# The last layer's final normalization, moved beside the last two experts of a mixture-of-experts encoder

## The chip, the core and the metric

The kernel runs on one core of a Trainium2 chip. A core has a matrix engine (PE, with its weight loads PEld), a vector engine (DVE), a scalar engine (ACT), a general engine (POOL) and a queue for transfers (SP), each with an instruction queue of its own that runs in order; sixteen DMA engines move data between memory and the core. Times are microseconds (us). The metric is the device time of one execution. Of the profile, the span reaches from the first to the last instruction.

## What is computed

Two layers of an encoder over 1024 tokens of 1024 features. Each layer is a mixer, a layer norm, a mixture of experts with 16 experts of which every token takes two, and another layer norm. What matters here is the end of the second layer:

```python
x = layer_norm(ALPHA * x + mixed @ w_out[i], ln_g[i, 0], ln_b[i, 0])
x = layer_norm(ALPHA * x + moe(x, ...), ln_g[i, 1], ln_b[i, 1])
# moe, per expert e and its tokens: (silu(xb @ w_gate[e]) * (xb @ w_up[e])) @ w_down[e], times the token's weight, summed per token
```

## The kernel before

`tail(layer, ...)` is the end of a layer: the output projection, the experts (`moe`), a loop for experts with more tokens than their places (`moe_rest`, none in this run's trace), and in the last layer `last_norm`, the final layer norm.

`moe` runs over the experts in the order 0, 8, 1, 9, ... 7, 15 (`SEQ`). Experts 0 to 7 have places for 192 tokens, a main part of 128 (`la`, `xa`, `ya`) and an extra part of 64 (`lb`, `xb`, `yb`); experts 8 to 15 have 128. For an expert its tokens' rows are gathered from memory (`gather`), transposed on PE and split into a high and a low part (`xah`, `xal`, and `xbc` for the extra part), multiplied with the gate and up weights (`gate_up`, PSUM tiles `dense`), passed through silu and the product on ACT and DVE (`ha`, `hb`), transposed again (`hposes`, tile `rtr`, then `hah`, `hal`, `hbc`), and multiplied with the down weights (`down`, PSUM tiles `rlg`, two buffers). ACT scales the result by the tokens' weights (`ya`, L2249; DVE for `yb`), and POOL issues an accumulating scatter of these rows into `accd` in memory (L2251, L2270), which already holds ALPHA * x. Each scatter waits for the one before it. `expert_weights` streams 1 MB weight tiles through SP into four raw buffers (`w_raw`); ACT and DVE split each (L77, L78) into one of five pairs `w_hi`, `w_lo`. PE works on expert n's gate and up weights and then on expert n-1's down weights; so the end of the program's work on PE is gate and up of expert 15, down of expert 7 (main, then extra part), down of expert 15. `late` holds the evacuations that `flush()` issues after the next matmuls; `rest` holds a generator of which each `flush()` runs one step (before: only the sorting of the routes).

`last_norm` runs `moe_norm`, which plans eight tiles of 128 tokens on the engines by estimated costs. All eight tiles are loaded from `accd` (L2370). Tiles 0 and 2: statistics on DVE (L2402 to L2406), reciprocal deviation on POOL (L2430), mean and deviation applied on ACT (L2441), times ln_g and plus ln_b on POOL (L2444, L2447). The other six: sums on ACT (L2410 to L2421), variance and reciprocal deviation on POOL (L2425, L2430), and two fused passes on DVE (L2435, L2438). SP stores each tile (L2467).

## Time and profile before

| | us |
|---|---|
| median of three runs | 2092.78 (2091.72 to 2098.09) |
| the profiled execution: its time | 2094.94 |
| the profiled execution: its span | 2093.2 |
| last matmul of the last expert begins | 2041.52 |
| last accumulating scatter has landed | 2053.6 (2047.12 + 6.49) |
| last fused pass of the final norm ends | 2089.4 |

Over the whole span PE is busy 90%, DVE 69%, ACT 53%, POOL 30%. A number of a row is the start on the chip's clock from the beginning of the span, then a duration. A row's idle time is that of the row's engine just before it.

### The profile page before, as it was taken

What the parts mean: (1) busy time and instruction counts of PE and PEld (TensorE: products, weight loads), DVE (VectorE), ACT (ScalarE), POOL (GpSimd) and SP (SyncE); (2) the same over time, 40 slices, a digit from 0 to 9 for tenths busy, and PEclk for the clock granted to TensorE, in tenths of its full rate; (3) what the DMA queues carried; (4) which work ended last, traced back from release to release, by engine and by line L of the source; (5) the groups of instructions that cost most, each with busy time, mean ns of one, the idle gap of its engine ahead of it and who ended that gap; (6) DMA issues with size and microseconds to landing.
All of it is one profiled execution on the core that took longest, in us unless ns stands there. A gap on an engine that the chain in (4) does not pass through costs nothing. (4 is left out here: it accounts for less than half of the span.)

```text
span 2093.2 us, 28147 instructions
## 1 busy us (share of the span) xinstructions
PE 1880.4 (90%) x9910; PEld 1552.2 (74%) x9910; DVE 1443.1 (69%) x2605; ACT 1107.4 (53%) x1783; POOL 617.9 (30%) x479
## 2 busy tenths in 40 slices
PE   7999999988969999999489899998797899999990
PEld 6788888876757777777388777887575687777770
DVE  5465666767978777777476654279699787777764
ACT  4455555653336666666354565444333466666653
POOL 1132222324542222221220000075455322222215
PEclk9999999999969999999689999999898899999995
DMA  5442321215449999999532222112663699999965
GB/s 183 116 132 60 67 66 28 108 63 177 155 148 323 300 294 292 302 304 287 167 116 62 68 81 73 62 30 64 208 207 119 214 314 305 306 307 308 310 193 176
DMA packets 252980, 371.21 MB, mean 177 GB/s; under 512 B 47820, under 2 KB 120868, under 8 KB 252836
## 3 DMA queue, kind: packets, MB, share of 16 engines
q1 hardware_dynamic: 236404, 317.90, 46.6%
q0 software_dynamic: 15376, 49.38, 9.1%
q10 hardware_dynamic: 1056, 2.10, 0.3%
q8 instruction: 80, 1.31, 0.3%
q14 instruction: 64, 0.52, 0.1%
HBM read 300.43 MB, written 65.76 MB: 175 GB/s over the span
## 5 line engine op out<-in xcount | busy, mean ns | idle before, releaser
L78 DVE TENSOR_TENSOR w_lo<-w_raw,w_hi 128x2048 fp32r<-128x2048 f32 (+1 forms) x220 | 465.9, 2124 | 192.6 <-ACT w_hi L77 189.3
L77 ACT CAST w_hi<-w_raw 128x2048 fp32r<-128x2048 f32 (+1 forms) x224 | 396.9, 1779 | 61.3 <-DMA w_raw<-in_exp_w_gate_dram 36.0
L105 PE MATMUL dense<-xT_h,w_hi 128*128 128x512 f32 (+1 forms) x544 | 226.3, 416 | 0.9 <-ACT xT_h L192 0.9
L107 PE MATMUL dense<-xT_h,w_lo 128*128 128x512 f32 (+1 forms) x544 | 209.2, 385 | 1.7 <-DVE w_lo L78 1.7
L2251 POOL DMA_INDIRECT accd<-ya,la x30 | 82.9, 2764 | 432.8 <-ACT ya L2249 424.8
L106 PE MATMUL dense<-xT_l,w_hi 128*128 128x512 f32 (+1 forms) x544 | 208.9, 384 | 1.0 <-DVE xT_l L193 1.0
L105 PE MATMUL dense<-w_hi,xah 128*128 128x512 f32 x480 | 197.9, 412 | 0.0
L107 PE MATMUL dense<-w_hi,xal 128*128 128x512 f32 x480 | 189.9, 396 | 0.0
L106 PE MATMUL dense<-w_lo,xah 128*128 128x512 f32 x480 | 189.8, 395 | 0.0
L583 POOL TENSOR_TENSOR bias<-bias_raw,masks 128x352 f32<-128x352 f32 (+1 forms) x96 | 85.3, 894 | 173.0 <-DVE att_st L349 153.0
L105 PE MATMUL dense<-w_hi,yh 128*128 128x512 f32 x288 | 122.7, 426 | 10.6 <-ACT yh L1839 10.6
L350 DVE TENSOR_SCALAR att_p<-att_p,att_st 128x256 f32<-128x256 f32 (+2 forms) x160 | 126.7, 792 | 5.7
L341 ACT ACTIVATE att_p<-att_p,att_st 128x352 f32<-128x352 f32 (+1 forms) x96 | 57.9, 603 | 129.1 <-DVE att_st L339 126.9
L107 PEld LDWEIGHTS dense<-xT_h,w_lo 128*128 128x128 f32 x544 | 104.1, 191 | 23.2 <-DVE w_lo L78 2.5
L107 PE MATMUL dense<-w_hi,yl 128*128 128x512 f32 x288 | 116.4, 404 | 1.4 <-DVE yl L1772 1.4
L106 PE MATMUL dense<-w_lo,yh 128*128 128x512 f32 x288 | 116.1, 403 | 0.0
L106 PEld LDWEIGHTS dense<-xT_l,w_hi 128*128 128x128 f32 x544 | 104.8, 193 | 8.4 <-DVE xT_l L193 1.4
L105 PEld LDWEIGHTS dense<-xT_h,w_hi 128*128 128x128 f32 x544 | 104.6, 192 | 8.4 <-ACT xT_h L192 1.0
L107 PEld LDWEIGHTS dense<-w_hi,xal 128*128 128x128 f32 x480 | 90.4, 188 | 21.8
L105 PEld LDWEIGHTS dense<-w_hi,xah 128*128 128x128 f32 x480 | 90.3, 188 | 18.7
L106 PEld LDWEIGHTS dense<-w_lo,xah 128*128 128x128 f32 x480 | 90.8, 189 | 17.8
L105 PE MATMUL rlg<-w_hi,hah 128*128 128x512 f32 x256 | 104.0, 406 | 0.0
(451 smaller groups left out, 4544.4 us busy)
## 6 DMA issues: line engine op xcount, KB each, us to landing
w_raw<-in_exp_w_gate_dram SPq DMA_DIRECT2D x64, 1024.0 KB, 9.2
w_raw<-in_exp_w_up_dram SPq DMA_DIRECT2D x64, 1024.0 KB, 9.9
w_raw<-in_exp_w_down_dram SPq DMA_DIRECT2D x62, 1024.0 KB, 7.6
w_raw<-in_na_w_in_dram SPq DMA_DIRECT2D x20, 512.0 KB, 3.8
w_raw<-in_w_out_dram SPq DMA_DIRECT2D x8, 1024.0 KB, 9.4
x1d<-z SPq DMA_DIRECT2D x16, 512.0 KB, 2.6
accd<-za SPq DMA_DIRECT2D x16, 512.0 KB, 3.9
z<-accd SPq DMA_DIRECT2D x16, 512.0 KB, 6.6
```

What stands on the lines that cost most here:

```text
L77: self.nc.scalar.copy(h[:, :n], t[:, :n])
L78: (eng or self.nc.vector).tensor_tensor(l[:, :n], t[:, :n], h[:, :n].bitcast(F), op=OP.subtract)
L105: nc.tensor.matmul(out, lhsT=a[0], rhs=b[0], start=first, stop=False)
L106: nc.tensor.matmul(out, lhsT=a[0], rhs=b[1], start=False, stop=False)
L107: nc.tensor.matmul(out, lhsT=a[1], rhs=b[0], start=False, stop=last)
L341: nc.scalar.activation(self.p, self.p, AF.Exp, bias=st[:, 0:1], scale=-1.0, accum_out=st[:, 1:2])
L350: nc.vector.tensor_scalar(self.p, self.p, st[:, 2:3], None, op0=OP.mult)
L583: nc.gpsimd.tensor_tensor(b[:, :nr], rev[:, w0:w0 + nr, u0:u0 + 32], nb.masks[:, half * 3 + kind].rearrange("p (a b) -> p a b", b=32)[:, :nr],
L2251: nc.gpsimd.indirect_dma_start(out=accd[layer], out_offset=bass.IndirectOffsetOnAxis(ap=la[:, 0:1], axis=0), in_=ya, in_offset=None, compu ...
```

## The change

In the last layer the scatters of the last two experts (X = 7 and Y = 15) into `accd` are left out, and `last_norm` with them. A class `Fin` takes their place. Its generator `steps` hangs in `rest`, so that each `flush()` from the down part of expert 14 on (the third from the end) runs one step. `loads` reads the eight tiles of `accd`, without X's and Y's parts, two at a time into raw weight buffers as these come free; each tile is normalized and stored to the output while X and Y are computed. `gathers` reads the `accd` rows of X's tokens (`zB`, 128 rows, and `zB2`, 64) and of Y's (`zA`, 128). X's results are added to `zB` and `zB2` on POOL (`main`, `extra`). Tokens that X and Y share are completed in `merge`: two 128x128 tiles of zeros and ones (`m`, from `merges`) multiply X's results, split in high and low parts, on PE, and DVE adds the product to `zA`; `last` adds Y's result to `zA`. The 320 rows are normalized as well and scattered to the output (`scatter`), over what the tiles' stores put there, with row numbers worked out in `prep`. `keep` stores X's and Y's results to `ysum`, and `beyond` runs what stood there before (their accumulation, `moe_rest`, `last_norm`) where an expert has more tokens than places. The splitting of weights may run one tile further ahead at the end (`ENDS`).

```diff
-    def moe(layer, rpool, ws, ereg):
+    def moe(layer, rpool, ws, ereg, fin=None):
...
+            X, Y = seq[-2:]
...
+            ENDS = 4 if fin else 3
...
-                while ws.raw and len(ws.ready) < min(AHEAD, 5 - len(early.w)):
+                while ws.raw and len(ws.ready) < min(AHEAD if ws.todo else ENDS, 5 - len(early.w)):
...
                     def evac(n=n, pa=pa):
+                        if fin and i == Y:
+                            fin.last(n, pa, la)
                         nc.scalar.mul(ya[:, n * 512:n * 512 + 512], pa, la[:, 1:2].bitcast(F))
-                        if n == 1:
+                        if fin and i in (X, Y):
+                            fin.main(i, n, ya, la)
+                        elif n == 1:
...
+                        if fin and i == X:
+                            fin.extra(n, yb, lb)
+                        elif n == 1:
...
+                if fin and n == NE - 2:
+                    fin.open(pool, lists, rest)
...
+                if fin and n == NE - 2:
+                    fin.gathers()
...
+            if fin:
+                fin.end()
...
+        def open(self, pool, lists, rest):
+            X, Y = SEQ[-2:]
+            self.pool, self.la, self.lb, self.ly = pool, lists[X][0], lists[X][1], lists[Y][0]
+            rest.append(self.steps())
...
+        def merges(self):
+            p = bank("rtr", 2)
+            nc.tensor.transpose(p[:, 0:128], self.f[:, 0:1].to_broadcast([128, 128]), ident)
+            self.m = [self.fz.tile([128, 128], R, name=f"fm{j}") for j in range(2)]
+            for j in range(2):
+                nc.vector.tensor_scalar(self.m[j], p[:, 0:128], self.f[:, 1 + j:2 + j], None, op0=OP.is_equal)
...
+        def gathers(self):
+            def get(name, n, idx):
+                t = self.pool.tile([n, D], F, name=name, tag=name, bufs=2 if name == "xa" else 1)
+                nc.gpsimd.indirect_dma_start(out=t, out_offset=None, in_=accd[self.layer],
+                                             in_offset=bass.IndirectOffsetOnAxis(ap=idx[:n, 0:1], axis=0))
+                return t
+            self.zB, self.zB2, self.zA = get("xa", 128, self.la), get("xb", 64, self.lb), get("xa", 128, self.ly)
...
+        def main(self, i, n, y, l):
+            if i == SEQ[-1]:
+                if n == 1:
+                    self.keep(y, l, 128)
+                return
+            sl = slice(n * 512, n * 512 + 512)
+            if n == 0:
+                self.yh, self.yl = [self.pool.tile([128, 8, 128], R, name=x, tag=x, bufs=2).rearrange("p a b -> p (a b)")
+                                    for x in ("xah", "xal")]
+            nc.scalar.copy(self.yh[:, sl], y[:, sl])
+            nc.gpsimd.tensor_tensor(self.yl[:, sl], y[:, sl], self.yh[:, sl].bitcast(F), op=OP.subtract)
+            nc.gpsimd.tensor_tensor(self.zB[:, sl], self.zB[:, sl], y[:, sl], op=OP.add)
+            if n == 1:
+                self.keep(y, l, 128)
...
+        def extra(self, n, y, l):
+            sl = slice(n * 512, n * 512 + 512)
+            if n == 0:
+                self.y2 = self.pool.tile([128, 8, 128], R, name="xbc", tag="xbc", bufs=1).rearrange("p a b -> p (a b)")
+            nc.scalar.copy(self.y2[0:64, sl], y[:, sl])
+            nc.vector.tensor_sub(self.y2[64:128, sl], y[:, sl], self.y2[0:64, sl].bitcast(F))
+            nc.gpsimd.tensor_tensor(self.zB2[:, sl], self.zB2[:, sl], y[:, sl], op=OP.add)
+            if n == 1:
+                self.keep(y, l, 64)
...
+        def keep(self, y, l, n):
+            k = len(self.sums)
+            lk = self.fz.tile([n, 2], I32, name=f"fl{k}")
+            nc.vector.tensor_copy(lk, l[:n])
+            nc.sync.dma_start(ysum[k, :n], y)
+            self.sums.append((k, lk, n))
...
+        def merge(self):
+            for n in range(2):
+                sl = slice(n * 512, n * 512 + 512)
+                p = bank("dense", 4)
+                for k, (m, y) in enumerate(((0, self.yh), (0, self.yl), (1, self.y2))):
+                    nc.tensor.matmul(p, lhsT=self.m[m], rhs=y[:, sl], start=k == 0, stop=k == 2)
+                nc.vector.tensor_add(self.zA[:, sl], self.zA[:, sl], p)
...
+        def stats(self, z, n, half=None):
+            if half == 1:
+                st = self.half
+            else:
+                st = self.fz.tile([128, 2, 6], F, name="fst", tag="fst" if half is None else "fsh", bufs=2)
+            for h in (0, 1) if half is None else (half,):
+                nc.vector.bn_stats(st[:n, h], z[:, h * 512:h * 512 + 512])
+            if half == 0:
+                self.half = st
+                return
+            mv = self.fz.tile([128, 5], F, name="fmv", tag="fmv", bufs=12)[:n]
+            nc.vector.bn_aggr(mv[:, 0:2], st[:n])
+            nc.vector.tensor_scalar(mv[:, 1:2], mv[:, 1:2], EPS, None, op0=OP.add)
+            nc.vector.tensor_scalar(mv[:, 2:3], mv[:, 0:1], -1.0, None, op0=OP.mult)
+            nc.gpsimd.tensor_tensor(mv[:, 3:4], mv[:, 1:2], mhalf[:n], op=OP.pow)
+            return mv
...
+        def fused(self, z, n, mv):
+            nc.vector.scalar_tensor_tensor(z, z, mv[:, 2:3], self.rows["ln_g"][:n], op0=OP.add, op1=OP.mult)
+            nc.vector.scalar_tensor_tensor(z, z, mv[:, 3:4], self.rows["ln_b"][:n], op0=OP.mult, op1=OP.add)
...
+        def last(self, n, p, l):
+            sl = slice(n * 512, n * 512 + 512)
+            nc.vector.scalar_tensor_tensor(self.zA[:, sl], p, l[:, 1:2].bitcast(F), self.zA[:, sl], op0=OP.mult, op1=OP.add)
+            self.mA = self.stats(self.zA, 128, n)
...
+        def scatter(self, z, n, j):
+            nc.gpsimd.indirect_dma_start(out=self.dst, out_offset=bass.IndirectOffsetOnAxis(ap=self.oi[:n, j:j + 1], axis=0),
+                                         in_=z, in_offset=None, bounds_check=S - 1, oob_is_err=False)
...
+        def loads(self):
+            while len(self.z) < 8 and len(self.z) // 2 < ws_free(self.ws):
+                i = self.ws.n % self.ws.raw_bufs
+                self.ws.n += 1
+                pair = self.ws.raw_pools[i].tile([128, self.ws.elems], F, tag=f"w_raw{i}", name="w_raw", bufs=1)
+                for k in range(2):
+                    t = len(self.z)
+                    self.z[t] = pair[:, k * D:k * D + D]
+                    r = TR + TILES[self.layer].index(t) * 128
+                    nc.sync.dma_start(self.z[t], accd[self.layer][r:r + 128])
...
+        def act_stats(self, t):
+            mv = self.mv[t] = self.fz.tile([128, 5], F, name="fmv", tag="fmv", bufs=12)
+            nc.scalar.activation(self.junk(), self.z[t], AF.Identity, accum_out=mv[:, 0:1])
+            nc.scalar.mul(mv[:, 2:3], mv[:, 0:1], -1.0 / D)
+            nc.scalar.activation(self.junk(), self.z[t], AF.Square, bias=mv[:, 2:3], accum_out=mv[:, 0:1])
+            nc.gpsimd.tensor_scalar(mv[:, 1:2], mv[:, 0:1], 1.0 / D, EPS, op0=OP.mult, op1=OP.add)
+            nc.gpsimd.tensor_tensor(mv[:, 3:4], mv[:, 1:2], mhalf, op=OP.pow)
...
+        def by_dve(self, t):
+            self.fused(self.z[t], 128, self.mv[t])
+            self.store(t)
...
+        def act_norm(self, t, n=128):
+            nc.scalar.activation(self.z[t], self.z[t], AF.Identity, bias=self.mv[t][:, 4:5], scale=self.mv[t][:, 3:4])
...
+        def by_pool(self, t, n=128):
+            for k, op in (("ln_g", OP.mult), ("ln_b", OP.add)):
+                nc.gpsimd.tensor_tensor(self.z[t], self.z[t], self.rows[k][:n], op=op)
+            if t not in ("B", "B2"):
+                self.store(t)
...
+        def steps(self):
+            self.z, self.mv = {}, {}
+            self.prep()
+            yield
+            self.merges()
+            yield
+            yield
+            yield
+            self.loads()
+            yield
+            self.loads()
+            yield
+            self.loads()
+            yield
+            self.loads()
+            self.dve_stats(0)
+            yield
+            self.loads()
+            self.act_norm(0)
+            self.act_stats(1)
+            yield
+            self.by_pool(0)
+            yield
+            self.by_dve(1)
+            self.act_stats(2)
+            yield
+            self.dve_stats(3)
+            yield
+            self.act_norm(3)
+            self.by_dve(2)
+            yield
+            self.by_pool(3)
+            self.act_stats(4)
+            yield
+            self.merge()
+            self.z["B"], self.z["B2"] = self.zB, self.zB2
+            self.dve_stats("B")
+            yield
+            self.act_stats(5)
+            self.act_norm("B")
+            self.by_dve(4)
+            self.dve_stats("B2", 64)
+            yield
+            self.by_pool("B")
+            self.act_stats(7)
+            self.act_norm("B2", 64)
+            self.dve_stats(6)
+            yield
...
+        def end(self):
+            self.by_dve(5)
+            self.by_pool("B2", 64)
+            self.by_dve(7)
+            self.by_dve(6)
+            self.fused(self.zA, 128, self.mA)
+            for z, n, j in ((self.zB, 128, 1), (self.zB2, 64, 2), (self.zA, 128, 0)):
+                self.scatter(z, n, j)
...
+        def beyond(self):
+            nb = nc.values_load(rt.blk[0:1, 32:33], min_val=0, max_val=16)
+            with tc.If(nb > 0):
+                with sbuf_scope("fb") as pool:
+                    for k, l, n in self.sums:
+                        y = pool.tile([n, D], F, name=f"fy{k}")
+                        nc.sync.dma_start(y, ysum[k, :n])
+                        nc.gpsimd.indirect_dma_start(out=accd[self.layer], out_offset=bass.IndirectOffsetOnAxis(ap=l[:, 0:1], axis=0),
+                                                     in_=y, in_offset=None, compute_op=OP.add)
+                moe_rest(self.layer, nb)
+                last_norm(self.layer, self.dst, self.rows)
...
-            moe(layer, tl.rpool, tl.ws, er[0])
+            fin = Fin(layer, dst, rows, gp, tl.ws) if dst is not None else None
+            moe(layer, tl.rpool, tl.ws, er[0], fin)
...
-        moe_rest(layer)
-        if dst is not None:
-            last_norm(layer, dst, rows)
+        if fin:
+            fin.beyond()
             gscope.__exit__(None, None, None)
+        else:
+            moe_rest(layer)
         tl.close()
```

ACT, from the last expert's silu on; `fmv` are a tile's statistics, `w_raw` here a tile to be normalized, `fjunk` a discarded output. Before:

```order
L77 CAST w_hi_18008<-w_raw_17909 128x2048
L77 CAST w_hi_18024<-w_raw_17939 128x2048
L77 CAST w_hi_18047<-w_raw_17963 128x2048
L2159 ACTIVATE ha_18028<-dense_17946 128x512
L2249 ACTIVATE ya_18031<-rlg_18034,la_16964 128x512
L192 CAST hah_18029<-rtr_18067 128x512
L2249 ACTIVATE ya_18031<-rlg_18053,la_16964 128x512
```

and now:

```order
L2168 ACTIVATE ha_18079<-dense_17972 128x512
L2662 ACTIVATE w_raw_17995<-w_raw_17995,fmv_18073 128x1024
L2645 ACTIVATE fjunk_18102,fmv_18101<-w_raw_17995 128x1024
L2646 ACTIVATE fmv_18101<-fmv_18101 128x1
L2647 ACTIVATE fjunk_18105,fmv_18101<-w_raw_17995,fmv_18101 128x1024
L2260 ACTIVATE ya_18082<-rlg_18085,la_16965 128x512
L2559 CAST xah_18123<-ya_18082 128x512
L2645 ACTIVATE fjunk_18135,fmv_18134<-w_raw_18021 128x1024
L2646 ACTIVATE fmv_18134<-fmv_18134 128x1
L2647 ACTIVATE fjunk_18138,fmv_18134<-w_raw_18021,fmv_18134 128x1024
L193 CAST hah_18080<-rtr_18142 128x512
L2260 ACTIVATE ya_18082<-rlg_18109,la_16965 128x512
```

Between silu (`ha`) and the cast of the transposed `ha` (`hah`), where one evacuation stood, there now stand tile 0's pass and two tiles' statistics as well.

POOL, after the last accumulating scatter that is left (that of the third expert from the end, the first row of before). Before, with the semaphores that a row waits for (DMASW numbers are those of POOL's transfers, in turn):

```order
L2251 DMA accd1_74<-ya_17891,la_16760 1216x1024 [waits DMASW3_49,Activation_49]
L2251 DMA accd1_74<-ya_18031,la_16964 1216x1024 [waits DMASW4_49,Activation_49]
L2270 DMA accd1_74<-yb_18032,lb_16975 1216x1024 [waits DMASW6_49,DMASW5_49,DVE_49]
L2251 DMA accd1_74<-ya_18101,la_17168 1216x1024 [waits DMASW7_49,DMASW6_49,Activation_49]
L2316 TENSOR_LOAD blk_15593 [waits DVE_49]
```

and now, without those, after the three gathers and tile 0's reciprocal deviation:

```order
L2648 TENSOR_SCALAR fmv_18101<-fmv_18101 128x1
L2649 TENSOR_TENSOR fmv_18101<-fmv_18101,mhalf_67 128x1
L2560 TENSOR_TENSOR xal_18124<-ya_18082,xah_18123 128x512
L2561 TENSOR_TENSOR xa_17963<-xa_17963,ya_18082 128x512
L2666 TENSOR_TENSOR w_raw_17995<-w_raw_17995,ln_g2_14955 128x1024
L2666 TENSOR_TENSOR w_raw_17995<-w_raw_17995,ln_b2_14957 128x1024
L2648 TENSOR_SCALAR fmv_18134<-fmv_18134 128x1
L2649 TENSOR_TENSOR fmv_18134<-fmv_18134,mhalf_67 128x1
L2560 TENSOR_TENSOR xal_18124<-ya_18082,xah_18123 128x512
L2561 TENSOR_TENSOR xa_17963<-xa_17963,ya_18082 128x512
L2607 TENSOR_TENSOR fmv_18168<-fmv_18168,mhalf_67 128x1
L2641 TENSOR_TENSOR fmv_18168<-fmv_18168 128x1
```

The accumulating scatters are gone, and POOL has statistics, X's additions (`xal`, `xa`) and tile 0's two passes in one row ahead of tile 3's reciprocal deviation (the last two rows).

POOL's end now, with semaphores (DMAHW numbers are those of SP's transfers):

```order
L2666 TENSOR_TENSOR xb_17965<-xb_17965,ln_g2_14955 64x1024 [waits Activation_49]
L2666 TENSOR_TENSOR xb_17965<-xb_17965,ln_b2_14957 64x1024 [waits Pool_49]
L2621 DMA out_0_dram<-xa_17963,foi_17933 1024x1024 [waits DMAHW4_49,DMAHW5_49,DMAHW3_49,DMAHW7_49,DMAHW2_49,DMAHW0_49]
L2621 DMA out_0_dram<-xb_17965,foi_17933 1024x1024 [waits DMASW0_49,Pool_49]
L2621 DMA out_0_dram<-xa_17967,foi_17933 1024x1024 [waits DMASW1_49,DVE_49]
L2731 TENSOR_LOAD blk_15594 [waits DVE_49]
```

The first scatter waits for the stores of the tiles, the second for DMASW0, the first's semaphore, and the third for DMASW1, the second's.

## Rows read from the trace of the kernel before

**Rows 1.** The busy time of each engine in four stretches of the end of the span (us; for each engine the busy us and the instructions that began there, then the granted clock of TensorE as a share of full speed, the DMA engines' share and the bytes moved).
```profile
core 0: us, PE busy (x) PEld busy (x) DVE busy (x) ACT busy (x) POOL busy (x), PEclk, DMA share, GB/s
2030.00:2042.00 12.00, 10.03 (x44) 7.85 (x44) 4.85 (x7) 3.08 (x6) 1.74 (x2) 1.00 0.29 44
2042.00:2060.00 18.00, 0.00 (x0) 0.00 (x0) 1.65 (x5) 1.09 (x2) 2.82 (x2) 0.58 0.54 128
2060.00:2089.40 29.40, 0.00 (x0) 0.00 (x0) 23.72 (x18) 16.82 (x32) 25.39 (x20) 0.50 0.54 217
2089.40:2093.20 3.80, 0.00 (x0) 0.00 (x0) 0.00 (x0) 0.00 (x0) 0.00 (x0) 0.50 0.34 138
```

**Rows 2.** Pieces of the chain that ended last (start us, us, what).
```profile
2041.82 1.43 DMA accd<-yb,lb
...
2047.12 6.49 DMA accd<-ya,la
...
2055.29 4.79 DMA z<-accd
...
2088.11 1.28 DVE z L2438
```

**Rows 3.** The timeline of ACT, DVE and PE around the last expert (start us, us, engine, line, operation; in brackets the idle time before it and what ended it).
```profile
2027.01 1.91 ACT L77 CAST w_hi<-w_raw 128x2048 fp32r<-128x2048 f32 x1 [4.14 <-DMA w_raw<-in_exp_w_down_dram]
2032.58 0.59 ACT L192 CAST hah<-rtr 128x512 fp32r<-128x512 f32 x1 [2.60 <-PE rtr L2215]
...
2028.94 2.29 DVE L78 TENSOR_TENSOR w_lo<-w_raw,w_hi 128x2048 fp32r<-128x2048 f32 x1 [3.76 <-ACT w_hi L77]
2031.15 0.68 DVE L2160 TENSOR_TENSOR ha<-ha,dense 128x512 f32<-128x512 f32 x1
...
2036.13 0.40 PE L105 MATMUL rlg<-w_hi,hah 128*128 128x512 f32 x1
...
2041.52 0.40 PE L107 MATMUL rlg<-w_hi,hal 128*128 128x512 f32 x1
```

**Rows 4.** The timeline of the final normalization, DVE and POOL beside each other, columns as in Rows 3.
```profile
2062.27 2.35 POOL L2444 TENSOR_TENSOR z<-z,ln_g 128x1024 f32<-128x1024 f32 x1 [1.35 <-ACT z L2441]
2062.53 0.68 DVE L2403 BATCH_NORM_STATS2 ln_st<-z 128x6 f32<-128x512 f32 x1
2063.61 2.09 DVE L2435 SCALAR_TENSOR_TENSOR z<-z,ln_mv,ln_g 128x1024 f32<-128x1024 f32 x1
...
2066.36 2.34 POOL L2447 TENSOR_TENSOR z<-z,ln_b 128x1024 f32<-128x1024 f32 x1
2066.42 3.36 DVE L2438 SCALAR_TENSOR_TENSOR z<-z,ln_mv,ln_b 128x1024 f32<-128x1024 f32 x1 [0.71 <-POOL ln_mv L2430]
2068.66 1.53 POOL L2430 TENSOR_TENSOR ln_mv<-ln_mv,mhalf 128x1 f32<-128x1 f32 x1
...
2086.61 1.47 POOL L2430 TENSOR_TENSOR ln_mv<-ln_mv,mhalf 128x1 f32<-128x1 f32 x1
```

**Rows 5.** The same stretch, one tile's statistics on DVE and POOL and another's on ACT, and one row of the whole span's groups by line and shape (busy us, mean ns of one | idle before).
```profile
2058.28 0.69 DVE L2402 BATCH_NORM_STATS2 ln_st<-z 128x6 f32<-128x512 f32 x1 [20.11 <-DMA z<-accd]
2059.60 0.21 DVE L2404 BATCH_NORM_AGGREGATE ln_mv<-ln_st 128x2 f32<-128x12 f32 x1
2060.08 0.57 POOL L2430 TENSOR_TENSOR ln_mv<-ln_mv,mhalf 128x1 f32<-128x1 f32 x1 [11.39 <-DMA z<-accd]
2060.73 0.19 POOL L2432 TENSOR_TENSOR ln_mv<-ln_mv 128x1 f32<-128x1 f32 x1
2060.96 1.24 ACT L2441 ACTIVATE z<-z,ln_mv 128x1024 f32<-128x1024 f32 x1 [0.26 <-POOL ln_mv L2432]
2077.19 1.06 ACT L2410 ACTIVATE junk<-z 128x1024 f32<-128x1024 f32 x1
2079.66 0.19 ACT L2421 ACTIVATION_READ_ACCUMULATOR junk<-z,ln_mv 128x1 f32 x1
...
L1256 POOL TENSOR_TENSOR dmat<-dmat,sT 128x512 f32<-128x512 f32 x16 | 20.3, 1266 | 29.3 <-ACT dmat L1250 19.8 <-PE io L1274 9.4
```

**Rows 6.** The issues of the last accumulating scatters (POOL's timeline, 2012 to 2048 us), and DMA issues with KB each and median us to landing (of 2069 to 2093.2 us, and of 2030 to 2053 us).
```profile
2013.63 2.90 POOL L2251 DMA_INDIRECT accd<-ya,la  x1 [16.36 <-ACT ya L2249]
2041.82 1.43 POOL L2270 DMA_INDIRECT accd<-yb,lb  x1 [6.22 <-issue]
2047.12 1.56 POOL L2251 DMA_INDIRECT accd<-ya,la  x1 [3.87 <-issue]
...
out_dram<-z SPq DMA_DIRECT2D x8, 512.0 KB, 2.6
...
accd<-yb,lb POOLq DMA_INDIRECT x1, 4.6
```

**Rows 7.** Busy time and DMA traffic by the microsecond, in the first and the last of the four microseconds in which the last accumulating scatter moved its bytes, and in the two of the last store, columns as in Rows 1.
```profile
2049.00:2050.00 1.00, 0.00 (x0) 0.00 (x0) 0.00 (x0) 0.00 (x0) 0.00 (x0) 0.50 1.11 86
...
2052.00:2053.00 1.00, 0.00 (x0) 0.00 (x0) 0.00 (x0) 0.00 (x0) 0.00 (x0) 0.50 0.49 94
2090.00:2091.00 1.00, 0.00 (x0) 0.00 (x0) 0.00 (x0) 0.00 (x0) 0.00 (x0) 0.50 0.77 315
2091.00:2092.00 1.00, 0.00 (x0) 0.00 (x0) 0.00 (x0) 0.00 (x0) 0.00 (x0) 0.50 0.52 209
```

**Rows 8.** The landing of the scatter issued at 2013.63 us (DMA issues of 2012 to 2015 us, columns as in Rows 6).
```profile
accd<-ya,la POOLq DMA_INDIRECT x1, 10.9
```

More of the change, by code (lines that the diff above doesn't have):

```diff
@@ L188, in body @@
     ydram = dram.tile([8, 128, S], F, name="ydram")
+    ysum = dram.tile([3, 128, D], F, name="ysum")
     def split_from_psum(h, l, p, scale=None):
@@ L2098, in load_list @@
                 if i < NXP:
-                    b = pool.tile([64, 2], I32, name="lb", tag="lb", bufs=8)
-                    nc.sync.dma_start(b, listd[layer][bass.ds(base + 128, 64)] if i else listd[layer][128:192])
+                    b = pool.tile([128, 2], I32, name="lb", tag="lb", bufs=8)
+                    for r in (0, 64) if fin and i == X else (0,):
+                        nc.sync.dma_start(b[r:r + 64], listd[layer][bass.ds(base + 128, 64)] if i else listd[layer][128:192])
+                    if not (fin and i == X):
+                        b = b[:64]
                 lists[i] = (a, b)
@@ L2533, in _consts @@
     import numpy as np
-    rows = np.zeros((128, 80), np.float32)
+    rows = np.zeros((128, 96), np.float32)
     i = np.arange(16)
```

44 lines of the change are left out of this document (38 added, 6 removed).

## The prediction

> **What bounds the kernel now.** I read the stretches of the end first [rows 1], then the chain that ended last [rows 2]. PE's work ends at 2041.9 [rows 3]; of the 51.3 us from there to the span's end, 18 go to the last accumulating scatters, one waiting for the other (4.6 us to landing for 64 rows, 6.49 for 128), and to the first load of the tiles [rows 1, 2, 6], and 29.4 to the final normalization, in which DVE is busy 23.7 us and POOL 25.4 [rows 1]. The timeline shows what that stretch is made of [rows 4]: DVE's fused pass alone takes 1.28 us [rows 2], but the one that begins at 2063.61 takes 2.09 and ends 1.08 after POOL's pass has (2062.27 + 2.35), and the one at 2066.42 takes 3.36, ending 1.08 after POOL's (2068.70). POOL's own step at 2068.66, 0.57 elsewhere [rows 5], takes 1.53, over the DVE pass that had just got its turn. DVE's statistics at 2062.53 keep their 0.68 under POOL's pass. So passes of POOL and DVE passes with two on-chip inputs take turns. The end is bound by the sum of both, not by the larger.
>
> The Trainium skill says the same in "SBUF — State Buffer", "Who interferes with whom": a DVE instruction with two SBUF inputs and a GpSimd one that reads SBUF share one port, and the second to start is blocked for the whole of the first. This speaks against the change, which gives POOL more such work. By that rule the sum comes to 2103.0 as below; were DVE and POOL free of each other, it would come to 2090.2.
>
> **How I count.** I go through the new instruction rows of each engine in order, each instruction starting when its engine is free and its inputs are there, with durations from rows: 2.66 us for ACT's sum, mean and squares of a tile (2077.19 to 2079.85), 1.24 for ACT's pass, 1.8 from the first DVE statistics of a tile to POOL, 0.57 + 0.19 for reciprocal deviation and product on POOL [rows 5], 2.3 for a POOL pass of 1024 [rows 4], 1.27 for one of 512 (the nearest row, another operation of that size) [rows 5], 1.14 for a fused DVE pass (between 1.08 and 1.28), 0.68 for a DVE step of 512 [rows 3]. POOL and two-input DVE steps take turns, first come first served. Counted in this way, the tail before ends on POOL at 2088.4 and on DVE at 2090.7; the rows say 2088.1 and 2089.4 [rows 2, 4].
>
> **Ahead of the last expert** little moves. The tiles may be loaded only once the scatter issued at 2013.63 has landed, 10.9 us later, at 2024.5 [rows 6, 8]; that is when the last weights are nearly in (the split on ACT begins at 2027.01 [rows 3]), so I charge the new loads and the three gathers nothing. They land from about 2029 on, in time for a DVE that is busy splitting weights until 2031.2 [rows 3]. On SP they stand behind the last weights, and only stores stand behind them. Row numbers and the two tiles of zeros and ones cost DVE some ten small steps in an idle gap, the copies to `ysum` fall into a stretch in which the DMA engines are busy 0.29 of the time [rows 1], and PE's seven added matmuls of at most 0.4 us [rows 3] fall where PE waits: nothing; without these covers they would cost some 2, 4 and 3 us.
>
> **Entry: 9 us lost on ACT.** On DVE, tile 0's statistics now stand ahead of the product `ha`, which ends at 2033.5 instead of 2031.8 [rows 3]. ACT stands still from 2029.4 until tile 0's deviation has gone through DVE and POOL, 2033.8; then tile 0's pass (1.24), tile 1's sums (2.66), one evacuation and one cast (1.25), tile 2's sums (2.66), and only then the cast `hah` that PE needs: done at 2042.2, against 2033.2 before [rows 3]. DVE's `hal` and the free PSUM buffer follow, so PE starts the last down products at 2045.4 instead of 2036.1. Queued behind ACT's wait are also the evacuations that free PSUM for expert 7's extra part.
>
> **Middle: POOL 16.6 us for one tile.** From tile 1's squares (2037.7; a fused pass of DVE goes first, to 2038.9) POOL's row up to tile 3's product is: short steps 0.8, expert 7's first half 2 x 1.27, tile 0's passes 2 x 2.3, short steps 0.8, second half 2 x 1.27, short steps 0.8; 12.0 in sum. DVE's two-input steps in between (three fused passes and two of 512, 4.6) take turns with it: 2055.5. ACT waits there for tile 3's pass, and behind it in ACT's row stand the copy and the cast of the second half of the extra part. Their last product reaches PE's `merge` at 2060.5; PE's last twelve matmuls stand behind it. They end at about 2064.8 instead of 2041.9. PE itself is not the limit, though: DVE comes to these results at 2072.
>
> **End of the passes.** From 2060.5 POOL still has six passes (tiles 3, B and B2: 13.8 us), DVE ten fused ones (tiles 4, 5, 7, 6 and A: 11.4); by turns 25.2, and 5.9 for POOL's twelve short steps and for waits on ACT: POOL ends at 2089.3, DVE ends tile 6 at 2087.0 and A at 2091.6. So of the 29.4 us of passes that were to be hidden, most come back, because the change adds POOL and DVE work: eight POOL passes instead of four, six half ones, fourteen fused ones instead of twelve.
>
> **Stores and scatters.** Tile 6's store is issued at 2087.1 and lands 2.6 later [rows 6]. Then three scatters, one after the other by their semaphores. The trace has no plain scatter of such rows. Upper bound: the accumulating ones, 6.49 + 5.3 (from 2041.82 to the next issue at 2047.12) + 6.49 = 18.3 [rows 2, 6]. Lower bound: a store's 2.6 each, 7.8 [rows 6]. An accumulating one of 128 rows moves bytes for some 3.6 us, a store of as many rows for 1.3 [rows 7]; with 2.3 us less for 128 rows and half of that for 64, 6.49 becomes 4.2 and 5.3 becomes 4.1: 12.5 for the three, my value, between the ends because only the moving of bytes should shrink. By the fixed 2 us and 436 bytes per ns of the Trainium skill, "DMA: Bandwidth & Descriptors", "Anatomy of one DMA", three such transfers would be an estimated 9 us; no run here shows it.
>
> **Sum.** 2087.1 + 2.6 + 12.5 + 1.2 (what lies behind the last landing before: DMA traffic ends within 2091 to 2092 [rows 7], the span at 2093.2) = 2103.4, against a span of 2093.2: +10.2. The profiled execution took 2094.94 with its span, the median of the runs is 2092.78; the change of the span goes onto the median: **2103.0**. Its own range: scatters -4.7 to +5.8, the count of the rows +-3: 2095.3 to 2111.8.
>
> **Rivals.** First, turns cost less than I count, because steps fall beside each other. With none at all the same count brings tile 6 to 2074.2, POOL to 2075.8, the end to 2074.3 + 2.6 + 12.5 + 1.2 = 2090.6: -2.6 us, 2090.2; with the short scatters -7.3, 2085.5. For it: the steps are more mixed with PSUM ones, which need no turn; against it: the turns are plain in rows 4, and the count holds for the tail before.
>
> Second, the other side: the early tiles really hide. If the tiles' first steps ran in ACT's and POOL's idle time before 2042 (ACT is busy 3.1 of 12 us there, POOL 1.7 [rows 1]) and PE still ended near 2042.6, the tail would be DVE's last statistics (1.8), eight fused passes (9.1) and B2's two on POOL (4.6): 2058.1, then 2.6 + 12.5 + 1.2: 2074.4, -18.8 us, 2074.0. It decides on tile 0: it would have to be through POOL before PE needs `hah`, at 2032; the first loads may start only at 2024.5 and DVE is taken until 2031.2, which speaks against it.
>
> Third, the fallback in `beyond` runs and the whole normalization is done again: the 53.6 to 2093.2 of before on top, some 2142.6. The trace before shows no expert with more tokens than places.
>
> **Chances.** Forecast 0.66 (0.06 of it inside the 0.3%, with the short scatters), first rival 0.24 (0.16 inside, 0.08 faster), second 0.06, longer scatters beyond my bounds or the fallback 0.04. 0.3% (6.3 us), about what a measurement here can tell from no change, puts the marks at 2086.5 and 2099.1: faster 0.14, same 0.22, slower 0.64. The range goes from 2087, which takes in the first rival's middle, to 2112; outside lie the second rival, the first's fast end and the long scatters, some 0.18.
>
> **What would show it.** After the change the cast `hah` of the last expert should stand at about 2042 on ACT, with an idle stretch of 4 us ahead of tile 0's pass; PE's last matmul at about 2065, waiting for DVE's extra product; DVE's fused passes often 2 to 3.4 us long; POOL's last pass at about 2089; three scatters of about 4 us each in a row from 2090. If PE ends near 2045, entry and middle are wrong; if the passes end before 2078, the turns; if the scatters overlap, the end.

## The result, and the profile after

| | us |
|---|---|
| median of four runs of the changed kernel | 2109.65 (2108.12 to 2109.96) |
| median of four runs of the kernel before, beside them | 2092.25 (2091.70 to 2098.09) |
| ratio, with its 95% interval | 1.0075 (1.0057 to 1.0094) |
| the profiled execution after: its time, its span | 2108.12, 2106.3 |

The change costs 0.75%, some 15.7 us. The place in the span at which the last part begins wanders by several us from run to run, with the same code too: the last weight split on ACT begins at 2027.01 in [rows 3], at 2026.16 in a second profiled run of the kernel before. Two runs are therefore compared below from the start of that split to the end of the span. This **tail** is 66.2 us in the profile of before (2093.2 - 2027.01) and 65.7 in the second (2091.9 - 2026.16). After the change it is 2106.3 - 2024.93 = 81.4.

The timeline of the profiled run after, around the last two experts; start us, us, engine, line, operation, in brackets the idle time before and what ended it (the rows that answer to [rows 3]):

```profile
2024.93 1.91 ACT L77 CAST w_hi<-w_raw 128x2048 fp32r<-128x2048 f32 x1 [3.81 <-DMA w_raw<-in_exp_w_down_dram]
2031.76 1.24 ACT L2662 ACTIVATE w_raw<-w_raw,fmv 128x1024 f32<-128x1024 f32 x1 [4.43 <-POOL fmv L2641]
...
2039.23 0.56 ACT L193 CAST hah<-rtr 128x512 fp32r<-128x512 f32 x1
...
2044.02 0.63 PE L105 MATMUL rlg<-w_hi,hah 128*128 128x512 f32 x1
...
2052.58 1.24 ACT L2662 ACTIVATE w_raw<-w_raw,fmv 128x1024 f32<-128x1024 f32 x1 [8.11 <-POOL fmv L2641]
...
2056.21 3.50 DVE L2570 TENSOR_TENSOR xbc<-yb,xbc 64x512 fp32r<-64x512 f32 x1 [0.68 <-ACT xbc L2569]
2059.24 2.70 POOL L2666 TENSOR_TENSOR w_raw<-w_raw,ln_b 128x1024 f32<-128x1024 f32 x1
2059.74 2.22 DVE L2579 COPY fl<-lb 64x2 int32<-64x2 int32 x1
2059.77 0.79 PE L2589 MATMUL dense<-xbc,fm 128*128 128x512 f32 x1 [9.64 <-DVE xbc L2570]
...
2064.02 0.40 PE L107 MATMUL rlg<-w_hi,hal 128*128 128x512 f32 x1
```

ACT stands 4.43 us for tile 0's deviation, and `hah` begins 14.3 us behind the split, where it was 5.6 before. It stands 8.11 us for tile 3's, while POOL has a row of other work. The second half of the extra part waits behind that, PE waits 9.64 us for it, and its last matmul begins 39.1 us behind the split (14.5 before).

The granted clock of TensorE in two stretches after the change, columns as in [rows 1]:

```profile
2036.00:2044.00 8.00, 7.34 (x16) 5.30 (x17) 7.00 (x11) 5.64 (x12) 7.84 (x6) 0.50 0.33 131
2059.00:2062.00 3.00, 2.23 (x5) 1.82 (x6) 2.97 (x3) 0.00 (x0) 2.87 (x2) 0.50 0.03 5
```

The clock was at its lower level (0.50, 1.2 GHz) from about 2032 on, after PE had stood 3.75 us, and again after the wait of 9.64 us; before the change it was 1.00 from 2030 to 2042 [rows 1]. At 0.50 one product of 512 columns began 0.43 us behind the other, at 1.00 it was 0.23.

The end of the passes, columns as above (it answers to [rows 4]):

```profile
2073.69 2.34 POOL L2666 TENSOR_TENSOR xa<-xa,ln_b 128x1024 f32<-128x1024 f32 x1
2073.95 2.10 DVE L2579 COPY fl<-la 128x2 int32<-128x2 int32 x1
...
2080.21 3.21 POOL L2666 TENSOR_TENSOR xb<-xb,ln_g 64x1024 f32<-64x1024 f32 x1
2081.13 3.36 DVE L2611 SCALAR_TENSOR_TENSOR w_raw<-w_raw,fmv,ln_g 128x1024 f32<-128x1024 f32 x1
2083.49 3.20 POOL L2666 TENSOR_TENSOR xb<-xb,ln_b 64x1024 f32<-64x1024 f32 x1
2084.60 3.18 DVE L2612 SCALAR_TENSOR_TENSOR w_raw<-w_raw,fmv,ln_b 128x1024 f32<-128x1024 f32 x1
...
2089.08 1.28 DVE L2612 SCALAR_TENSOR_TENSOR xa<-xa,fmv,ln_b 128x1024 f32<-128x1024 f32 x1
```

Tile 6's two passes each begin under a pass of POOL and end about 1.1 us after it (2083.42 and 2084.49; 2086.69 and 2087.78). The copy of two columns at 2073.95 waits for POOL's pass too.

The chain that ended last (start us, us, what), and behind it the busy time by stretches, columns as in [rows 1] (they answer to [rows 2, 7]):

```profile
2091.61 3.45 DMA out_dram<-xa,foi
...
2095.88 2.47 DMA out_dram<-xb,foi
...
2099.24 0.87 POOL out_dram L2621
```

```profile
2101.00:2102.00 1.00, 0.00 (x0) 0.00 (x0) 0.00 (x0) 0.00 (x0) 0.00 (x0) 0.50 0.62 246
2102.00:2106.30 4.30, 0.00 (x0) 0.00 (x0) 0.00 (x0) 0.00 (x0) 0.00 (x0) 0.50 0.00 0
```

The landings of the same stretch (issues with KB each and median us to landing, as in [rows 6]):

```profile
out_dram<-w_raw SPq DMA_DIRECT2D x4, 512.0 KB, 2.6
...
out_dram<-xa,foi POOLq DMA_INDIRECT x2, 3.3
```

Three scatters follow one another, 4.27 and 3.25 us from issue to issue. The last bytes move before 2102; 4.3 us in which nothing moves and no engine is busy end the span. Before, 1.2 us lay there from the end of the microsecond with the last bytes [rows 7], and 1.6 us from these bytes themselves, the last of which move at 2091.63.

### The profile page after: what moved, and what is told of

It is laid out like the page before. It is cut to its first block, busy times and chain, and to the rows that moved or that the text cites. A ratio compares the mean times of both kernels' runs of the same rounds, so it can differ in the third digit from the quotient of the medians.

```text
span 2106.3 us, 28186 instructions
## 1 busy us (share of the span) xinstructions
PE 1885.6 (90%) x9917; PEld 1555.3 (74%) x9917; DVE 1464.3 (70%) x2646; ACT 1108.4 (53%) x1784; POOL 635.1 (30%) x496
## 5 line engine op out<-in xcount | busy, mean ns | idle before, releaser
L106 PEld LDWEIGHTS dense<-w_lo,xah 128*128 128x128 f32 x480 | 90.4, 188 | 17.4
```

Source lines behind the costliest of these rows:

```text
L106: nc.tensor.matmul(out, lhsT=a[0], rhs=b[1], start=False, stop=False)
```

## The experiments

All of them, with the tail read as above. The ratio is that to the kernel before in the same set of runs.

| kernel | last split | span | tail | ratio (95% interval) |
|---|---|---|---|---|
| before, `before_again` | 2027.01, 2026.16 | 2093.2, 2091.9 | 66.2, 65.7 | 1 |
| changed, `change_again` | 2024.93, 2024.42 | 2106.3, 2105.6 | 81.4, 81.2 | 1.0075 (1.0057 to 1.0094), 1.0060 (1.0047 to 1.0074) |
| `passes_on_dve` | 2022.70 | 2096.5 | 73.8 | 1.0042 (1.0025 to 1.0059) |
| `steps_later` | 2020.88 | 2099.3 | 78.4 | 1.0063 (1.0042 to 1.0085) |
| `no_fallback` | 2025.59 | 2106.8 | 81.2 | 1.0082 (1.0061 to 1.0102) |
| `no_scatters` | 2020.27 | 2087.9 | 67.6 | 1.0009 (1.0000 to 1.0019) |
| `both` | 2026.52 | 2100.8 | 74.3 | 1.0036 (1.0022 to 1.0050) |
| `rows_behind_tiles` | 2021.56 | 2091.7 | 70.1 | 1.0014 (1.0003 to 1.0025) |
| `a_by_store` | 2024.61 | 2102.5 | 77.9 | 1.0052 (1.0035 to 1.0070) |
| `before_on_dve` | 2022.10 | 2082.9 | 60.8 | 0.9979 (0.9969 to 0.9989) |
| `tiles_first` | 2024.66 | 2086.4 | 61.7 | 0.9974 (0.9965 to 0.9983) |
| `before_act_stats` | 2026.99 | 2089.8 | 62.8 | 0.9980 (0.9971 to 0.9989) |

**Is it the tail at all?** Two runs without an edit.

> The changed kernel as it is, once more, beside the others on the same chip. It asks how much of the 17.4 us between the medians lies ahead of the last weight split, where nothing was moved that any reading shows: the split began on ACT at 2024.93 in the profiled run of the change, at 2027.01 in the one of before, at 2020.3 to 2026.5 in the variants. Theory: that place wanders by some 3 us from run to run, and the change costs what the tail shows, 81.4 against 66.2 us: 15 us, 2106 to 2110. Rival: the larger number of prepared weights or the longer lists make the kernel slower ahead of the split as well; then the split begins 2 us or more later than in before on the mean.

> The kernel before, one more look at its tail: from the start of the last weight split on ACT to the end of the span it took 66.2 us. Theory: 66.2 again within 0.5 us, wherever the split begins. Rival: the tail itself wanders by some us, and the comparison by it is no better than that by the span.

The split in the second run of the kernel before:

```profile
2026.16 1.91 ACT L77 CAST w_hi<-w_raw 128x2048 fp32r<-128x2048 f32 x1 [4.15 <-DMA w_raw<-in_exp_w_down_dram]
```

The changed kernel's split begins no later than that of before (over all the runs of the table it begins between 2020.27 and 2027.01), and both tails repeat within 0.5 us. So the cost lies behind the split: 81.3 - 66.0 = 15.3 us on the mean, where the two ratios give 12.6 and 15.7.

**The turns: POOL's passes on DVE.**

```diff
         def by_pool(self, t, n=128):
             for k, op in (("ln_g", OP.mult), ("ln_b", OP.add)):
-                nc.gpsimd.tensor_tensor(self.z[t], ...)
+                nc.vector.tensor_tensor(self.z[t], ...)
```

> The changed kernel, but the gain and bias passes of tiles 0 and 3 and of the row sets B and B2 (eight in all) are issued on DVE instead of POOL; nothing else is moved. Theory, turns: POOL passes and DVE passes with two on-chip inputs exclude each other, so each of the eight costs about 1.14 us in place of 2.3 of the shared turns; 9.3 us of turns fall away, DVE's passes stop stretching to 2 to 3.4 us, ACT's wait for tile 3's deviation (8.1 us) shrinks by some 4, and the passes end some 6 to 10 us earlier: time about 2102 (2099 to 2105) where the changed kernel took 2109.65. Rival, no turns (the stretched passes come from something else): DVE, busy 49.9 of the 62 us from 2029 on and without idle time from 2061.9, has 9.1 us more to do and the end moves later by 5 to 9 us: about 2116.

The tail shrinks by 7.6 us although DVE has eight passes more. Its timeline:

```profile
2022.70 1.91 ACT L77 CAST w_hi<-w_raw 128x2048 fp32r<-128x2048 f32 x1 [4.17 <-DMA w_raw<-in_exp_w_down_dram]
...
2043.16 1.25 ACT L2662 ACTIVATE w_raw<-w_raw,fmv 128x1024 f32<-128x1024 f32 x1
...
2067.66 0.16 DVE L2579 COPY fl<-la 128x2 int32<-128x2 int32 x1
2070.30 1.21 DVE L2666 TENSOR_TENSOR xb<-xb,ln_g 64x1024 f32<-64x1024 f32 x1
...
2079.23 1.28 DVE L2612 SCALAR_TENSOR_TENSOR xa<-xa,fmv,ln_b 128x1024 f32<-128x1024 f32 x1
```

ACT no longer waits for tile 3, the copy takes 0.16 us where it took 2.10, and the last pass ends 57.8 us behind the split (65.4 in the changed kernel). The rival without turns would have made it slower; it is out.

**The waits in ACT's row.** All steps from tile 0's statistics on come later; `merge()` is moved ahead of `dve_stats(3)`, so that it keeps its place ahead of the last expert's sums, and `end` first runs what is left of `steps`.

```diff
             self.loads()
+            yield
+            yield
+            yield
             self.dve_stats(0)
```

> The changed kernel, but all normalization steps from tile 0's statistics on stand three hooks later in the program (the product of the merge keeps its place ahead of the last expert's final accumulation), so that the cast hah, the evacuations and the casts of the extra part no longer stand behind ACT's steps for tiles 0, 2 and 3. Theory, head-of-line waits decide: PE ends near 2046 instead of 2064.4 and the passes end with it 12 us or more earlier: time about 2096 or less. Rival, the sum of turns decides: PE ends near 2046 too, but POOL and DVE have the same passes to do (some 44 us of exclusive ones and 6 of POOL's short steps) from about 2033 on, so the passes end only 3 to 8 us earlier, near 2084, and the time is about 2104 (2101 to 2107). A second rival: the steps put off leave DVE idle ahead of them and fall behind the end, no gain or up to 4 us later.

```profile
2026.45 0.59 ACT L193 CAST hah<-rtr 128x512 fp32r<-128x512 f32 x1 [1.95 <-PE rtr L2224]
...
2034.19 0.68 DVE L2280 TENSOR_TENSOR t<-rlg,t 64x512 f32<-64x512 f32 x1 [5.24 <-ACT t L2279]
...
2048.55 0.40 PE L107 MATMUL rlg<-w_hi,hal 128*128 128x512 f32 x1
```

`hah` is back at 5.6 us behind the split, PE's last matmul at 27.7 (39.1), and yet the tail is only 3.0 us shorter. Theory and rival both had PE end near 2046, some 21 us behind the split, which was too early; the gain is that of the rival, at the low end of its 3 to 8 us. An early end of PE is worth little by itself: the passes that wait for turns are the same ones. DVE also stands 5.24 us in front; what that takes from the gain was not tried apart. Both edits in one kernel:

> The changed kernel with both edits that made it faster: the eight gain and bias passes on DVE, and the normalization steps three hooks later. From the start of the last weight split on ACT to the end of the span the changed kernel took 81.4 us, with the passes on DVE 73.8, with the later steps 78.4, the kernel before 66.2. Theory, the sum of turns decides: the two gains overlap only where ACT waited for tile 3, so 70 to 72 us, time about 2097 (2094 to 2100). Rival: with POOL's passes gone DVE is the only bound and its rows begin later in this order, so the later steps bring nothing more: 73 to 75 us, about 2100.

The rival held: 74.3. Without POOL's passes DVE is the bound, and the shift leaves it idle in front:

```profile
2039.45 0.68 DVE L2280 TENSOR_TENSOR t<-rlg,t 64x512 f32<-64x512 f32 x1 [5.23 <-ACT t L2279]
...
2083.46 1.28 DVE L2613 SCALAR_TENSOR_TENSOR xa<-xa,fmv,ln_b 128x1024 f32<-128x1024 f32 x1
```

**The scatters and the ending.** Three kernels: the call of `scatter` in `end` left out; `fin.beyond()` left out; and

```diff
-            for z, n, j in ((self.zB, 128, 1), (self.zB2, 64, 2), (self.zA, 128, 0)):
+            for z, n, j in ((self.zB, 128, 1), (self.zB2, 64, 2)):
                 self.scatter(z, n, j)
+            nc.sync.dma_start(self.dst[0:128, :], self.zA)
```

> The changed kernel without the three final scatters: the rows of the last two experts' tokens are computed and normalized but not stored again, so these rows of the output stay incomplete. It prices the serial scatters: theory: the end then is the landing of tile 6's store (2090.4) or A's last pass (2090.4) with the ending of 3.9 us behind it, 2094.3 instead of 2106.3: 12 us less, time about 2097.5. Rival: part of the scatters lies beside the ending or beside the stores, and less than 9 us goes.

> The changed kernel without the fallback (the branch for experts with more tokens than places is left out; for this input nothing in it runs). It prices the ending: from the third scatter's landing at about 2102.4 to the end of the span at 2106.3 are 3.9 us, where before 1.2 lay behind the last landing. Theory: the branch over a body of code on all engines is what lies there, so the span shrinks by 2 to 3 us, time about 2107. Rival: the time belongs to the scatter itself (its completion is told later than its bytes move), and the span stays within 0.5 us of 2106.3.

> The changed kernel, but the third scatter (the rows A of the last expert) is replaced by a plain store of A over the first 128 rows of the output, behind the second scatter: these rows and the tokens of A are not what the reference has. It asks what the 4.3 us without any traffic are, from the last bytes of the third scatter to the end of the span (1.2 us before, 1.9 us with no scatters; leaving out the fallback did not change them). Theory: they belong to a late scatter, whose completion the program's end waits for on POOL's queue; then the end is a store's, 1.2 to 2 us behind its bytes, and the span is 2.5 to 4.5 us shorter. Rival: they belong to any program that scatters into the output near its end, and the span shrinks by less than 1.5 us.

Without scatters the tail is 13.8 us shorter, more than the 12 expected, since the ending shrinks with them. Without the fallback nothing changes: the branch is not what the last 4 us are. With a store as the last transfer the tail is 3.5 us shorter; the store is issued 0.1 us behind the second scatter's landing, where the third scatter began 0.8 us behind it, and its last bytes move 2.2 us behind its issue, those of the third scatter 2.8 us. The busy time around the last bytes, columns as above, in the kernel before, without the fallback, with the store at the end, and without scatters; for the last also the queue (packets, MB, share) that moved the bytes of its second stretch:

```profile
2091.70:2093.20 1.50, 0.00 (x0) 0.00 (x0) 0.00 (x0) 0.00 (x0) 0.00 (x0) 0.50 0.00 0
```

```profile
2102.50:2106.80 4.30, 0.00 (x0) 0.00 (x0) 0.00 (x0) 0.00 (x0) 0.00 (x0) 0.50 0.00 0
```

```profile
2100.00:2100.20 0.20, 0.00 (x0) 0.00 (x0) 0.00 (x0) 0.00 (x0) 0.00 (x0) 0.50 0.48 164
2100.20:2102.50 2.30, 0.00 (x0) 0.00 (x0) 0.00 (x0) 0.00 (x0) 0.00 (x0) 0.50 0.00 0
```

```profile
2085.00:2085.40 0.40, 0.00 (x0) 0.00 (x0) 0.40 (x1) 0.00 (x0) 0.00 (x0) 0.50 0.71 277
2085.40:2087.90 2.50, 0.00 (x0) 0.00 (x0) 0.31 (x1) 0.00 (x0) 0.00 (x0) 0.50 0.01 3
```

```profile
q14 instruction: 1, 0.01, 0.8%
```

The few bytes that still move behind 2085.40 without scatters are those of the instruction queue, not of a store. From the last bytes of the data, the span runs 4.3 us behind a scatter (4.4 without the fallback) and 2.4 us (store at the end) and 2.5 us (no scatters) behind a store; without scatters DVE's last pass, that of A, ends 2.2 us before the span does. The kernel before has 1.6, and 1.7 to 2.1 in its second run and its two variants. So some 2 us of the ending belong to a scatter that comes last; the 0.3 to 0.9 us that the changed kernel has on top with a store at its end stay open. What the program waits for there no row shows.

**The order of the end.** With the passes on DVE, the tiles first, each row set scattered as it comes (`by_pool("B")` moves here from `steps`):

```diff
             self.by_dve(5)
-            self.by_pool("B2", 64)
             self.by_dve(7)
             self.by_dve(6)
+            self.by_pool("B")
+            self.scatter(self.zB, 128, 1)
+            self.by_pool("B2", 64)
+            self.scatter(self.zB2, 64, 2)
             self.fused(self.zA, 128, self.mA)
-            for z, n, j in (...): self.scatter(z, n, j)
+            self.scatter(self.zA, 128, 0)
```

> The changed kernel with the eight passes on DVE, and with DVE's last work in another order: tiles 5, 7, 6, then the row sets B, B2 and A, each scattered as soon as it is ready. Theory: the first two scatters (4.3 us from issue to next issue for 128 rows, 3.25 for 64) then lie beside the passes of B2 and A, and of the 14.9 us from the first scatter's issue to the end of the span only A's landing, the ending and what the stores force stay: 4 us less than with the passes on DVE alone, 69 to 71 us from the last weight split, time about 2096. Rival: the scatters slow or are slowed by the passes beside them (their descriptors are made by POOL, whose steps wait for DVE's two-input passes elsewhere), and less than 2 us is gained.

70.1 us, as expected: two scatters lie beside passes. The first one's own instruction takes 2.06 us (1.09 elsewhere) beside DVE's last passes, which costs 1 us of it. The pass beside it had begun first; in `tiles_first` below, where the scatter begins at 2071.59 and the pass beside it at 2071.64, it keeps 1.09. So a scatter's instruction may take turns as well; only these two rows speak for it.

```profile
2075.49 1.22 DVE L2666 TENSOR_TENSOR xb<-xb,ln_b 64x1024 f32<-64x1024 f32 x1
...
2075.68 2.06 POOL L2621 DMA_INDIRECT out_dram<-xa,foi  x1 [9.89 <-DVE xb L2666]
2080.92 0.95 POOL L2621 DMA_INDIRECT out_dram<-xb,foi  x1 [3.18 <-DMA out_dram<-xa,foi]
2084.16 0.98 POOL L2621 DMA_INDIRECT out_dram<-xa,foi  x1 [2.29 <-DMA out_dram<-xb,foi]
```

**Versions that beat both.** `tiles_first` writes `steps` and `end` anew. In order: `dve_stats(0)`; `act_stats(1)`, `by_dve(0)`; `by_dve(1)`, `act_stats(2)`; `dve_stats(3)`; `by_dve(2)`; `by_dve(3)`, `act_stats(4)`; `merge()`, `act_stats(5)`; `by_dve(4)`, `act_stats(7)`; `by_dve(5)`, `act_stats(6)`; then in `end` `act_stats` of B and B2 on ACT, and on DVE tiles 7, 6, B, B2, A, each row set with its scatter.

> The change's idea with the causes found taken out: no pass on POOL and no normalization pass on ACT (ACT makes the statistics of tiles 1, 2, 4 to 7 and of the row sets B and B2, DVE those of tiles 0 and 3 and of A, every pass is a fused one of DVE), and all eight tiles ahead of the row sets, whose scatters go out as the sets come. Theory: DVE is the bound from 4 us behind the last weight split on; some 39 us of its work up to the last tile, then 3.7 us to the first scatter, 5.2 and 3.25 to the next two and 7.5 to the end, 19.7 in all: 62 to 65 us from the split, a little less than the 66.2 of before, time about 2090. Rival: ACT, with 24 us of statistics in one row with PE's evacuations, falls behind and DVE waits: 67 us or more, no better than before.

The two others change one call in the kernel before:

```diff
-moe_norm(..., (1, 3, 4, 5, 6, 7), rows=rows, fused=(1, 3, 4, 5, 6, 7), affine={0: 'pp', 2: 'pp'})
+moe_norm(..., (1, 3, 4, 5, 6, 7), rows=rows, fused=(1, 3, 4, 5, 6, 7), affine={0: 'vv', 2: 'vv'})   # before_on_dve
+moe_norm(..., range(1, 8), rows=rows, fused=range(1, 8), affine={0: 'vv'})                          # before_act_stats
```

> The kernel before, but the gain and bias passes of tiles 0 and 2 of the last normalization are issued on DVE instead of POOL. Theory, turns: four passes of 2.35 us of the shared turns become four of 1.14 to 1.28, so the stretch of 29.4 us shortens by 4 to 5 us, time about 2088. Rival, POOL and DVE free of each other: the longer of POOL's 25.4 and DVE's 23.7 busy us decides; DVE, whose passes then were never stretched, would take 23.7 + 4.6 = 28.3, and the end moves by -1 to +3 us: about 2093.

> The kernel before with no pass on POOL, and with the statistics of tile 2 on ACT as well, so that DVE makes the statistics of tile 0 alone, its two passes and seven fused pairs. With the passes of tiles 0 and 2 on DVE the tail took 60.8 us from the last weight split. Theory: DVE, without a gap from 2058 on there, has 1.8 us of statistics less, and ACT's seven tiles of 2.66 us keep up: 58 to 60 us, time about 2087. Rival: ACT now sets the pace (18.6 us and one pass behind the first load), and the tail stays at 60.5 us or more.

`before_on_dve`: 60.8, 5.4 less than before, as the turns say. Its split and one of the passes moved to DVE:

```profile
2022.10 1.91 ACT L77 CAST w_hi<-w_raw 128x2048 fp32r<-128x2048 f32 x1 [4.30 <-DMA w_raw<-in_exp_w_down_dram]
...
2066.14 1.22 DVE L2447 TENSOR_TENSOR z<-z,ln_b 128x1024 f32<-128x1024 f32 x1
```

`tiles_first`: 61.7, just under the 62 to 65 expected, and 20 us less than the change:

```profile
2024.66 1.91 ACT L77 CAST w_hi<-w_raw 128x2048 fp32r<-128x2048 f32 x1 [4.23 <-DMA w_raw<-in_exp_w_down_dram]
...
2063.90 1.28 DVE L2612 SCALAR_TENSOR_TENSOR w_raw<-w_raw,fmv,ln_b 128x1024 f32<-128x1024 f32 x1
...
2066.49 1.28 DVE L2612 SCALAR_TENSOR_TENSOR w_raw<-w_raw,fmv,ln_b 128x1024 f32<-128x1024 f32 x1
...
2071.59 1.09 POOL L2621 DMA_INDIRECT out_dram<-xa,foi  x1 [2.22 <-DVE xb L2611]
...
2079.09 0.98 POOL L2621 DMA_INDIRECT out_dram<-xa,foi  x1 [2.29 <-DMA out_dram<-xb,foi]
```

The last tile is done 43.1 us behind the split (62.9 in the changed kernel); the 18.6 us from there to the end are the store, the serial scatters and the ending. The ratios of the three overlap, so which of them is fastest is open. `before_act_stats` missed, and not through its rival: ACT is done 7 us ahead of DVE. In front DVE stands 2.18 us for ACT's pass of tile 0, and then each of its second passes waits for a short step of POOL:

```profile
2081.46 1.28 DVE L2438 SCALAR_TENSOR_TENSOR z<-z,ln_mv,ln_b 128x1024 f32<-128x1024 f32 x1 [0.44 <-POOL ln_mv L2430]
2081.51 1.28 POOL L2425 TENSOR_SCALAR ln_mv<-ln_mv 128x1 f32<-128x1 f32 x1
2082.87 1.47 POOL L2430 TENSOR_TENSOR ln_mv<-ln_mv,mhalf 128x1 f32<-128x1 f32 x1
2084.38 1.28 DVE L2438 SCALAR_TENSOR_TENSOR z<-z,ln_mv,ln_b 128x1024 f32<-128x1024 f32 x1 [0.44 <-POOL ln_mv L2430]
```

These steps take 0.2 to 0.6 us when nothing else runs [rows 5]; in a row of DVE passes without a gap each of them waits for a pass, and a tile costs 2.92 us (2081.46 to 2084.38) where it costs 2.59 in `tiles_first` (2063.90 to 2066.49).

## Why the prediction was right, and where its size was off

Slower, as forecast, and 2109.65 lies inside 2087 to 2112, near its upper end. The median moved by 17.4 us (16.9 against the 2092.78 that the forecast started from) and the tail by 15.3, where the forecast had 10.2. Its steps, in us behind the last weight split (forecast: minus 2027.01; measured: minus 2024.93):

| step | forecast | measured |
|---|---|---|
| entry: cast `hah` done | 15.2 | 14.9 |
| entry: PE's last down products begin | 18.4 | 19.1 |
| middle: product for tile 3 on POOL | 28.5 | 27.6 |
| middle: PE ends | 37.8 | 39.5 |
| end of passes: POOL | 62.3 | 61.8 |
| end of passes: DVE, tile 6 (its store is issued) / A | 60.1 / 64.6 | 62.9 / 65.4 |
| from tile 6 to the landing of its store | 2.6 | 2.6 |
| from there through three scatters | 12.5 | 11.9 |
| behind the last landing | 1.2 | 4.0 |

Ahead of the last expert: no sign of a cost, since the split begins no later (`change_again`). **Entry** and **middle** came as forecast in their waits and their order: ACT stood 4.43 us for tile 0 and 8.11 for tile 3. Not priced was TensorE's clock: the forecast has its added matmuls at most 0.4 us long, and at 0.50 those of expert 7's extra part took 0.63 to 0.80. Worked out from the rows, at the clock of before PE's last down products would have begun some 1.6 us earlier, at about 17.5, and PE would have ended some 1.4 us earlier; that 19.1 lies so near the 18.4 is partly luck. What the forecast also said there, that PE is not the limit, is shown by `steps_later`: PE 11.4 us earlier, the tail 3.0 shorter.

**End of passes**: the mechanism held (`passes_on_dve`, `before_on_dve`); tile 6 was 2.8 us late, and this is the first term that was mis-sized. In the forecast POOL's last pass, B2's second, ended 2.2 us behind tile 6; in the run it ended 1.1 us ahead of it, so one more pass of POOL had its turn before tile 6. Two things were not priced right there. A fused pass of DVE that waits for nobody takes 1.27 to 1.29 us and not 1.14. The copies of the index lists in `keep` on DVE had no price: the second and third take 2.22 and 2.10 us, where the third takes 0.16 without POOL's passes; the pass behind the third needs the same turn, so that copy itself can have cost little. How much of the 2.8 each makes was not tried apart.

**Stores and scatters**: 11.9 for 12.5, though made up otherwise: 1.2 us from the store's landing (2087.8 + 2.6) to the first scatter, landings of 3.45, 2.47 and some 3.15 (the median of the two of 128 rows is 3.3), and 0.8 between each two. The 9 us estimated from the Trainium skill, "DMA: Bandwidth & Descriptors", "Anatomy of one DMA", agree with the 9.1 of the three landings; the hand-overs of 2.8 come on top.

The second term that was mis-sized is the **last 1.2 us**, carried over from a program that ends on a store; it measured 4.0. Counted in the same way the changed kernel has 1.9 where it ends on a store (`a_by_store`: issued at 2097.98, landed at about 2100.6 with the 2.6 of the other stores, span 2102.5), so some 2.1 of the 2.8 belong to the scatter at the end; the cause of the other 0.7 stays open. 2.8 for tile 6, 2.8 for the ending and -0.6 for the scatters are the 5 us between the forecast's tail (2103.4 - 2027.01 = 76.4) and the measured one. What is left of the difference between the medians no trace shows: the profiled run of before was 2.2 us above the 2092.78, that of the change 1.5 below its median, and the other runs have no row that shows where their split began.

The first rival, turns that cost nothing, is out by `passes_on_dve` and `before_on_dve`. The second, early tiles that hide, is out for this order of instructions, since tile 0's deviation was through POOL at 2031.7 and ACT's pass and statistics still stood in front of `hah`. `tiles_first`, where DVE makes tile 0's passes alone and no wait for a deviation stands in ACT's row, gains 4 to 5 us on before, not the rival's 18.8; but its PE ends 31.3 us behind the split (14.9 before), so a run with early tiles and a PE that they do not hold up is not among these. The third, the fallback, did not run.

## What to carry to other kernels

Before work is moved beside other work, add up what the two engines that take turns have to do: here POOL's pass costs 2.3 us of the shared turns and DVE's 1.1 to 1.3, so giving passes to an idle POOL lengthens the end, and one changed call took 5.4 us from the tail of the kernel before. A step that waits in an in-order engine's row also holds up what stands behind it, but the first thing to find is what ends last after the wait is gone. A program that ends on scatters paid here for each hand-over between them and for a longer ending; put the last dependent ones beside other work.
